# A four-layer decoder trunk on one core: residual stream moved by blocks, value projections made wide, and the steps of the layer joins handed out anew

## The chip, the cores and the metric

The kernel runs on one core of a Trainium2 chip. Its engines work side by side and meet through semaphores: TensorE (PE in the profile, its weight loads PEld), VectorE (DVE), ScalarE (ACT), GpSimd (POOL), and SyncE (SP), which issues most of the DMAs. The metric is device microseconds of one execution. Before the change three runs took 2686.42, 2691.14 and 2692.78 us; the median is 2691.14.

## What is computed

A sequence of 1024 positions, 1024 wide, goes through four layers. Each layer normalises, scales and shifts, runs one mixer, gates its output, and adds to the stream:

```
mod = (c @ ada_w[i] + ada_b[i])[:, None, :]
shift, scale, gate = jnp.split(mod, 3, axis=-1)
h = rmsnorm(x, norm_g[i]) * (1.0 + scale) + shift
y = hgrn2_mixer | swa_mixer | gdn_mixer      # i % 3, layers 0..3: hgrn2, swa, gdn, hgrn2
x = x + gate * y
```

Every mixer has one input projection, a branch output that is multiplied by a SiLU gate from the same projection, and one output projection. HGRN2 (layers 0 and 3) is a gated linear recurrence with 8 heads of 128, projections q, f, v, z of 1024 columns each. SWA (layer 1) is attention in a window of 128 with 16 query heads, 4 key heads and a sink for each head. GDN (layer 2) is a gated delta rule with a causal convolution of four taps on q, k and v and 16 value heads. All of it is float32, and a product of a projection is made of three matmuls on a high and a low part (`mm3`, L204 to L206: hi·hi, lo·hi, hi·lo).

## The kernel before, in words

Activations stand feature-major: a tile `x` holds one half of the sequence (512 positions) as eight blocks of 128 features by 512 positions. Nearly everything is done for half 0 and then for half 1 (`hf`). The normalised and modulated input is held as a pair `hhi`, `hlo`, again eight blocks a half. It comes from `norm_stats` (squares, a row sum on PE, an rsqrt on DVE, and `n_rb`, the factor spread over all partitions) and `norm_apply` (L504 to L506: for each of eight blocks one DVE product into `n_t`, one ACT add of the shift into `hhi`, one DVE step into `hlo`).

Weights come by SP in tiles `w_raw` of 256 KB with three buffers, which the streamed modulation weights `ada_w` share; ACT makes `w_hi` and DVE `w_lo`. `proj_fm` multiplies feature-major (result `proj_ps`, 24 matmuls of 512 columns for one half of 128 features). `proj_tm` multiplies position-major for the values (result `projt_ps`, matmuls of 256 columns, L204 to L206).

What sets the order is a scheduler. The program is written as generators, `weave` takes from several of them by the costs that they yield, some stretches have a raised priority (`early`, `high_priority`), and the scheduler then orders each engine's instructions, which the engine works off strictly in that order. While the mixer of head h runs (`mix`, `scan`, `inverse`: short dependent chains), the projections of the next head fill PE.

The stages touched by the change:

- **Prologue** (ends with the first `proj_ps` at 55 us): x is loaded and transposed on PE (`load_x`, L310), and the shift and scale of layer 0 are made from four 2 MB parts of `ada_w` by `ada_first`, all four parts on PE (`ada_row`, L400).
- **HGRN2 mix** (`mix`, L1030 to L1147): three levels of small matmuls (`lev_ps`, L1040, and L1087 for the last level), diagonal copies by POOL (L1081), the recurrence (`o_ps`, `s_ps`), then the head's output is transposed on PE by four matmuls (`ot_ps`, L1136), gated by `zs` on DVE (L1139), and stored to the scratch `od` by SP (L1141).
- **SWA mix**: the scores, softmax, transposes `pt_ps`, and pairs of `pv_ps` matmuls, one pair after each transpose (L1374).
- **GDN projections**: `conv` evicts a projection by an ACT copy (L644) and an ACT product (L648), three DVE taps (L650) and a tanh; `trans` transposes the result on PE at once.
- **Joins**: at the end of a layer `out_mm` and `rest` add into x (L1216, L534). After a half is added, its norm for the next layer is issued whole. Between layers a whole half of x goes to and from DRAM by SP in one DMA of 2 MB (`spill_x`, `fill_x`).

PSUM has eight banks; three of them (`proj` twice, `ta` once; two inside GDN) take projections in turn, `lev` has two, `tr`, `s` and `o` one each.

## Time and profile before

| what | value |
|---|---|
| median of three runs | 2691.14 us |
| the profiled execution, its own time | 2695.95 us |
| its span | 2694.2 us |
| instructions in the profile | 51458 |
| DMA traffic | 273.29 MB, mean 101 GB/s |

The prediction's sums are made against the profiled execution. In a row of the timeline the first number is the start in us from the span's start and the second the duration; matmuls are pipelined, so durations overlap, and what one costs in a stream is the distance between two starts. In a row of waits the numbers are total us, times, and the longest. In a row of stretches (`A:B`) come the length, then busy us of PE, PEld, DVE, ACT and POOL, the granted TensorE clock, the DMA share and GB/s. In a row of the groups by line come busy us and mean ns, then idle us before it and what ended that.

### The profile page before, as it was taken

How to read it: one execution, taken by the hardware profiler on the slowest of the kernel's cores; microseconds unless marked ns; L12 is line 12 of the kernel's file. 1: busy time of each engine (PE TensorE's matmuls, PEld its weight loads, DVE VectorE, ACT ScalarE, POOL GpSimd, SP SyncE). 2: the span in 40 equal slices, each digit the busy share in tenths (PEclk: the TensorE clock that was granted, in tenths of full speed). 3: DMA queues.
4: the chain of work that ended last, by engine and by line, in shares of the span. 5: the costliest groups of instructions: out<-in, count | busy, mean ns of one | idle time of the engine just before them, and what ended most of it. 6: DMA issues, size and time to landing. Idle time of an engine off the chain costs nothing.

```text
span 2694.2 us, 51458 instructions
## 1 busy us (share of the span) xinstructions
PE 2609.7 (97%) x18927; PEld 2102.4 (78%) x18927; DVE 2010.2 (75%) x5619; ACT 1272.9 (47%) x3268; POOL 136.7 (5%) x352
## 2 busy tenths in 40 slices
PE   8999999999999999999999999999999999999998
PEld 4878878778878777677877777777788878787877
DVE  6776766788687877777988888989876766656575
ACT  4333333444454655454556556666644433333342
POOL 0000100000000000001001101100000000000000
PEclk9999999999999999999999999999999999999999
DMA  6332222344223252333343333333584221111133
GB/s 241 92 93 84 68 79 72 110 137 157 59 87 103 75 158 91 114 98 84 102 115 99 96 105 100 94 97 82 179 254 132 71 60 37 56 51 43 49 118 115
DMA packets 361490, 273.29 MB, mean 101 GB/s; under 512 B 70499, under 2 KB 294166, under 8 KB 361238
## 3 DMA queue, kind: packets, MB, share of 16 engines
q1 hardware_dynamic: 360950, 268.96, 33.9%
q8 instruction: 149, 2.44, 0.4%
q14 instruction: 103, 0.84, 0.1%
q0 software_dynamic: 288, 1.05, 0.1%
HBM read 224.77 MB, written 45.15 MB: 100 GB/s over the span
## 4 chain that ended last, share of the span: by engine, by line
PE 71%; DVE 17%; DMA 5%; ACT 3%; issue 3%; SPq 1%; POOL 0%; DVEq 0%; ACTq 0%; POOLq 0%
PE proj_ps L206 10%; PE proj_ps L205 9%; PE proj_ps L204 9%; PE outp_ps L204 5%; PE outp_ps L205 5%; PE outp_ps L206 5%; DMA ada_w<-in_ada_w_dram 3%; PE projt_ps L204 3%; PE projt_ps L206 3%; PE projt_ps L205 3%; DVE w_lo L180 2%; DVE gd_tb L650 2%; PE pv_ps L1374 1%; DVE ada_acc L413 1%; PE w_ps L890 1%
## 5 line engine op out<-in xcount | busy, mean ns | idle before, releaser
L204 PE MATMUL proj_ps<-hhi,w_hi 128*128 128x512 f32 x1664 | 675.8, 406 | 6.1 <-ACT gd_tb L648 5.9
L206 PE MATMUL proj_ps<-hhi,w_lo 128*128 128x512 f32 x1664 | 679.9, 409 | 0.0
L205 PE MATMUL proj_ps<-hlo,w_hi 128*128 128x512 f32 x1664 | 671.2, 403 | 0.0
L204 PEld LDWEIGHTS proj_ps<-hhi,w_hi 128*128 128x128 f32 x1664 | 315.3, 190 | 59.4 <-ACT gd_tb L648 6.3
L205 PEld LDWEIGHTS proj_ps<-hlo,w_hi 128*128 128x128 f32 x1664 | 314.7, 189 | 59.0 <-issue 2.4
L206 PEld LDWEIGHTS proj_ps<-hhi,w_lo 128*128 128x128 f32 x1664 | 315.0, 189 | 56.1 <-issue 1.0
L179 ACT CAST w_hi<-w_raw 128x512 fp32r<-128x512 f32 x332 | 202.0, 611 | 303.3 <-PE proj_ps L205 188.1
L180 DVE TENSOR_TENSOR w_lo<-w_raw,w_hi 128x512 fp32r<-128x512 f32 x332 | 223.1, 674 | 155.2 <-ACT w_hi L179 129.1
L205 PE MATMUL projt_ps<-w_lo,hhi 128*128 128x256 f32 x896 | 258.7, 291 | 4.7 <-DVE w_lo L180 4.7
L204 PE MATMUL projt_ps<-w_hi,hhi 128*128 128x256 f32 x896 | 257.8, 290 | 0.6 <-ACT w_hi L179 0.6
L206 PE MATMUL projt_ps<-w_hi,hlo 128*128 128x256 f32 x896 | 256.8, 290 | 0.0
L204 PE MATMUL outp_ps<-o_hi,w_hi 128*128 128x512 f32 x576 | 229.2, 400 | 4.7 <-ACT o_hi L1200 3.4
L205 PE MATMUL outp_ps<-o_lo,w_hi 128*128 128x512 f32 x576 | 229.4, 399 | 0.0
L206 PE MATMUL outp_ps<-o_hi,w_lo 128*128 128x512 f32 x576 | 226.8, 396 | 0.7 <-DVE w_lo L183 0.7
L205 PEld LDWEIGHTS projt_ps<-w_lo,hhi 128*128 128x128 f32 x896 | 171.1, 192 | 8.1 <-DVE w_lo L180 6.0
L204 PEld LDWEIGHTS projt_ps<-w_hi,hhi 128*128 128x128 f32 x896 | 171.1, 192 | 3.7 <-ACT w_hi L179 1.0
L206 PEld LDWEIGHTS projt_ps<-w_hi,hlo 128*128 128x128 f32 x896 | 170.8, 192 | 2.4 <-issue 1.0
L650 DVE SCALAR_TENSOR_TENSOR gd_tb<-gd_xs,taps,gd_tb 128x512 f32<-128x512 f32 x192 | 145.2, 756 | 28.3 <-ACT gd_tb L648 19.7
L182 ACT ACTIVATE w_hi<-w_raw,par 128x512 fp32r<-128x512 f32 (+1 forms) x136 | 94.3, 698 | 137.0 <-PE outp_ps L205 89.2
L204 PEld LDWEIGHTS outp_ps<-o_hi,w_hi 128*128 128x128 f32 x576 | 108.8, 189 | 29.1 <-ACT o_hi L1200 4.9
L413 DVE SCALAR_TENSOR_TENSOR ada_acc<-ada_w,par,ada_acc 128x512 f32<-128x512 f32 x140 | 104.8, 749 | 33.4 <-DMA ada_w<-in_ada_w_dram 32.5
L206 PEld LDWEIGHTS outp_ps<-o_hi,w_lo 128*128 128x128 f32 x576 | 108.7, 189 | 23.5 <-DVE w_lo L183 1.3
(398 smaller groups left out, 4894.8 us busy)
## 6 DMA issues: line engine op xcount, KB each, us to landing
ada_w<-in_ada_w_dram SPq DMA_DIRECT2D x160, 256.0 KB, 2.8
w_raw<-in_hg_in_w_dram SPq DMA_DIRECT2D x136, 256.0 KB, 2.8
w_raw<-in_gd_in_w_dram SPq DMA_DIRECT2D x108, 256.0 KB, 3.0
o_in<-od SPq DMA_DIRECT2D x72, 256.0 KB, 3.2
w_raw<-in_gd_out_w_dram SPq DMA_DIRECT2D x64, 256.0 KB, 2.9
w_raw<-in_sw_in_w_dram SPq DMA_DIRECT2D x48, 256.0 KB, 2.9
w_raw<-in_hg_out_w_dram SPq DMA_DIRECT2D x40, 256.0 KB, 2.8
ada_w<-in_ada_w_dram SPq DMA_DIRECT2D x8, 1024.0 KB, 9.2
```

Of the source, the lines that this page charges most:

```text
L179: nc.scalar.copy(hi, raw)
L180: nc.vector.tensor_tensor(lo, raw, hi.bitcast(F32), ALU.subtract)
L182: nc.scalar.activation(hi, raw, AF.Copy, scale=scale)
L204: mm(out, a[0], b[0], start=start, stop=False)
L205: mm(out, a[0], b[1], start=False, stop=False)
L206: mm(out, a[1], b[0], start=False, stop=stop)
L413: self.nc.vector.scalar_tensor_tensor(acc, w, c, acc, ALU.mult, ALU.add)
L650: nc.vector.scalar_tensor_tensor(y, xs[:, j:j + HT], w(j), y, ALU.mult, ALU.add)
L890: nc.tensor.matmul(po[:, hd[a]], dd["u"][a, hf][:, cs], rhs, start=True, stop=True)
L1374: nc.tensor.matmul(po[a * 64:(a + 1) * 64], vg[:, n + 1 - nkb + b, :], p4[:, :, a, :], start=b == 0, stop=b == nkb - 1)
```

## The change

- **Values of HGRN2**: `proj_v` is made of two wide pieces of four heads each by `proj_wide` (matmuls of 512 columns, `projw_ps`) and no longer of four pieces by `proj_tm`. The values live in the two slots of x, which are free between the joins; head 7 has tiles of its own.
- **HGRN2 output**: for heads 0 to 6 the four PE transposes and the gating at once give way to a DVE product, a DVE transpose in squares of 32, four stores of 64 KB to a scratch `pd` that put the squares in place, and, in the next half's mix, a load from `pd`, a DVE product with `zs` and the store to `od` (`gate`).
- **HGRN2 last level**: L1087's twelve matmuls (widths 96, 64, 32) become sixteen (32, 64, 64, 32 on four column groups), issued together by `tied`; the diagonal copies move from POOL to ACT. Projections are spread one head to a mix, z of a head beside q and f of the next.
- **SWA**: both transposes come first, and the four `pv_ps` matmuls then run together. The k projection's two tile pairs share one rsqrt, and the order of the first projections changes.
- **GDN**: the transposes after a convolution wait for the middle of the next projection (`turns`); the gates z of units 1 and 2, half 0, are made at the layer's start, and the list `ZL` hands out the rest.
- **Norm**: `n_t` stands in PSUM (`lev`). The norm of half 1 at a join is no longer issued whole at the join but kept (`k.last`) and issued by the next layer: at its beginning in HGRN2 and SWA, and in GDN four blocks after each of the first two convolutions.
- **Stream by blocks**: each block of x is stored by POOL's queue as soon as it is added (`keep_x`), and loaded by SP in 256 KB blocks inside `out_mm` (`due`).
- **Prologue**: half 0 of x, the four `ada_w` parts and the first weights are requested in one order; parts 2 and 3 are multiplied on PE, parts 0 and 1 on DVE (`ada_first` with and without a bank); the norm of half 0 follows by halves of its blocks; the rotary tables move into layer 0's mix.

The difference, cut to its core:

```diff
     def norm_apply(self, i, hf, rb):
...
-            t = self.np.tile([P, HT], F32, name="n_t", tag="n_t", bufs=NB["n_t"])
+            t = self.psum("lev", "n_t", 2)
...
+            yield 1
...
     def conv(dd, hf, ps, ct, out):
...
-            nc.scalar.copy(xs[:, 3:], ps)
+            with self.tc.issue_after(self.hold.ins) if self.hold else nullcontext():
+                nc.scalar.copy(xs[:, 3:], ps)
...
+            self.piece = None
+            with self.tc.issue_after(last.ins):
+                drain(take(self.last, self.parts))
+            self.hold = self.piece
...
-        self.early(proj_kq(0, ds[0], ((0,),)), EV)
-        self.spill_x(1)
+        self.parts = 4
+        self.early(chain(proj_kq(0, ds[0], ((0,),)), proj_z(1, ds[1], (0,)), proj_z(2, ds[2], (0,))), EV)
+        drain(self.last)
...
+    def proj_wide(self, ws, evac, tts):
+        for tt in tts:
+            ps = self.proj_ps("projw_ps")
+            hf, ts = tt // 4, slice((tt % 4) * P, (tt % 4 + 1) * P)
+            for k in range(KT):
+                self.mm3(ps, (self.hhi[hf][:, k, ts], self.hlo[hf][:, k, ts]), ws[k], k == 0, k == KT - 1)
...
         def mix(h, d, halves=(0, 1)):
...
-                            nc.gpsimd.tensor_copy(at[gs, :, gs], A[gs].rearrange("p (c t) -> p c t", c=NC))
+                            nc.scalar.copy(at[gs, :, gs], A[gs].rearrange("p (c t) -> p c t", c=NC))
...
+                    if l == 3 and pend:
+                        gate()
...
                 if h < HA:
-                    nc.sync.dma_start(od[h * P:(h + 1) * P, hf * HT:(hf + 1) * HT], of)
+                    nc.vector.tensor_tensor(v4(on, "b c"), v4(po, "c b"), r[:, :, None, None].to_broadcast([P, NC, 4, 32]), ALU.mult)
+                    ob = tl("tmp")
+                    nc.vector.transpose(ob, on)
...
+                        nc.sync.dma_start(dst[a], ob[a * 32:(a + 1) * 32].rearrange("q (b t) -> q b t", b=4))
+                    pend.append((h, hf, d["zs", hf]))
...
+        def gate():
+            h, hf, z = pend.pop()
...
+            nc.sync.dma_start(t, self.pd[rows])
+            nc.vector.tensor_tensor(v4(z, "c b"), v4(t, "b c"), v4(z, "c b"), ALU.mult)
+            nc.sync.dma_start(od[rows], z)
...
     def out_mm(self, i, w_out, k0, nk, hf, scale=None, last=False):
...
+            if (hf, j) in self.due:
+                self.due.remove((hf, j))
+                self.nc.sync.dma_start(*self.block(hf, j))
...
+    def keep_x(self, hf, j):
+        if self.more:
+            x, d = self.block(hf, j)
+            self.nc.gpsimd.dma_start(d, x)
```

What the scheduler makes of it stands here at three places. The first is DVE at the join into GDN (layer 2), from the factor of half 1's norm (`n_sq`) on; `n_t` and `hlo` are norm blocks, `gd_tb<-gd_xs` the taps that belong to an eviction of a projection. Before, up to the first taps:

```order
L504 SCALAR_TENSOR_TENSOR n_t<-x_11280,gcol,n_rb 128x512 x2
L506 SCALAR_TENSOR_TENSOR hlo<-n_t,mod,hhi 128x512
L180 TENSOR_TENSOR w_lo<-w_raw,w_hi 128x512
L506 SCALAR_TENSOR_TENSOR hlo<-n_t,mod,hhi 128x512
L504 SCALAR_TENSOR_TENSOR n_t<-x_11280,gcol,n_rb 128x512 x2
L180 TENSOR_TENSOR w_lo<-w_raw,w_hi 128x512
L506 SCALAR_TENSOR_TENSOR hlo<-n_t,mod,hhi 128x512 x2
L504 SCALAR_TENSOR_TENSOR n_t<-x_11280,gcol,n_rb 128x512 x2
L180 TENSOR_TENSOR w_lo<-w_raw,w_hi 128x512
L506 SCALAR_TENSOR_TENSOR hlo<-n_t,mod,hhi 128x512 x2
L650 SCALAR_TENSOR_TENSOR gd_tb<-gd_xs,taps,gd_tb 128x512 x2
```

And with the change:

```order
L519 TENSOR_TENSOR n_sq<-ident,rs_y 128x512
L190 TENSOR_TENSOR w_lo<-w_raw,w_hi 128x512
L690 SCALAR_TENSOR_TENSOR gd_tb<-gd_xs,taps,gd_tb 128x512
L595 TENSOR_TENSOR gd_wab<-w_raw,gd_wab 128x8x32
L690 SCALAR_TENSOR_TENSOR gd_tb<-gd_xs,taps,gd_tb 128x512
L190 TENSOR_TENSOR w_lo<-w_raw,w_hi 128x512
L690 SCALAR_TENSOR_TENSOR gd_tb<-gd_xs,taps,gd_tb 128x512
L533 SCALAR_TENSOR_TENSOR n_t<-x_11000,gcol,n_rb 128x512 x2
L697 SCALAR_TENSOR_TENSOR gd_k<-gd_tb 128x512
L535 SCALAR_TENSOR_TENSOR hlo<-n_t,mod,hhi 128x512 x2
L533 SCALAR_TENSOR_TENSOR n_t<-x_11000,gcol,n_rb 128x512 x2
```

Sixteen norm steps stood ahead of the first taps; now the first taps stand ahead of them, and four blocks follow each of the first two convolutions.

The second place is PE in the prologue, between the first `ada_row` and the first wide value projection. Before:

```order
L400 MATMUL ada_row<-ada_w_362,par 1x512 x7
L400 MATMUL ada_row<-ada_w_383,par 1x512
L449 MATMUL ada_ps<-ones,ada_acc 128x1 x4
L400 MATMUL ada_row<-ada_w_383,par 1x512 x7
L310 MATMUL x_ps<-ident,x_in 128x128 x9
L449 MATMUL ada_ps<-ones,ada_acc 128x1 x4
L310 MATMUL x_ps<-ident,x_in 128x128 x23
L265 MATMUL taps_ps<-ident,taps_in 128x128
L204 MATMUL proj_ps<-hhi,w_hi 128x512
```

With the change, from the last matmuls of the first piece of q and f on:

```order
L218 MATMUL proj_ps<-hhi,w_hi 128x512
L219 MATMUL proj_ps<-hlo,w_hi 128x512
L220 MATMUL proj_ps<-hhi,w_lo 128x512
L428 MATMUL ada_row<-ada_w_182,par 1x512 x6
L480 MATMUL ada_ps<-ones,ada_acc 128x1 x4
L326 MATMUL x_ps<-ident,x_in 128x128 x8
L218 MATMUL projw_ps<-w_hi,hhi 128x512
L326 MATMUL x_ps<-ident,x_in 128x128 x4
```

The first 24 matmuls of the q and f projections now stand ahead of the second `ada_row` part and of the transposes of x's half 1, where all of these stood ahead of the first projection.

The third place is SP's queue in the first heads of layer 0, with the stores of a head's output, the loads of the streamed `ada_w`, and the weights. Before:

```order
L177 DMA w_raw<-in_hg_in_w_dram 128x4x128 x2
L427 DMA ada_w<-in_ada_w_dram 128x512 x3
L1141 DMA od_76<-hg_tmp 128x512
L427 DMA ada_w<-in_ada_w_dram 128x512 x2
L177 DMA w_raw<-in_hg_in_w_dram 128x4x128 x2
```

With the change:

```order
L1218 DMA pd<-hg_tmp 32x4x128 x4
L458 DMA ada_w<-in_ada_w_dram 128x512 x3
L1097 DMA hg_tmp<-pd 128x512
L458 DMA ada_w<-in_ada_w_dram 128x512
L187 DMA w_raw<-in_hg_in_w_dram 128x4x128 x2
L1099 DMA od_76<-hg_zs 128x512
```

One store has become four stores, a load that must follow them, and a store that follows a DVE product; weight loads stand behind them in the same queue.

More of the change, by code (lines that the diff above doesn't have):

```diff
@@ L100, in __init__ @@
         self.x = [None, None]
-        self.oo, self.pre = {}, {}
+        self.oo, self.pre, self.last, self.parts, self.due, self.more = {}, {}, iter(()), 0, set(), True
+        self.piece = self.hold = self.turn = self.step = None
     def hslot(self, name):
@@ new lines, in ada_load, with ada_first @@
+    def ada_load(self, i, part):
+        w = self.ins["ada_w"][i].rearrange("(k p) n -> p k n", p=P)
+        wk = self.hslot("ada_w0").bitcast(F32)
+        for g in range(2):
+            self.nc.sync.dma_start(wk[:, 4 * g:4 * g + 4, :], w[:, 4 * g:4 * g + 4, part * HT:(part + 1) * HT])
+        return wk
+    def ada_first(self, i, part, acc, wk, bank):
+        nc = self.nc
+        if bank:
+            pr = self.psum(*bank)
+            for k in range(KT):
+                nc.tensor.matmul(pr[0:1, :], self.cT[:, k:k + 1], wk[:, k, :], start=k == 0, stop=k == KT - 1)
+            acc = acc[0:1, :]
+            nc.scalar.copy(acc, pr[0:1, :])
+        else:
+            for k in range(KT):
+                self.ada_step(acc, wk[:, k, :], k)
+        yield
+        with self.tc.issue_after(self.step.ins) if self.step else nullcontext():
@@ L1028, in mix @@
             for hf in halves:
[L1029 removed]
+                q, f, kg, qf = (d[x, hf] for x in ("q", "f", "kg", "qf"))
+                v = value(h, hf)
                 k0 = d["k0", hf]
@@ L1150, in hgrn2 @@
         ds = [dict() for _ in range(H)]
+        drain(self.last)
         gv = proj_v(0)
-        self.early(chain(proj(0, ds[0], "qf", (0,)), take(gv, 8)))
+        if i == 0:
+            for g, at, n, ew in ((proj(0, ds[0], "qf", (0,)), self.start[0], 80, EW), (take(gv, 16), self.start[1], 0, 50)):
+                self.early(g, eo=self.tc.cur_priority - at + n, ew=ew)
+            rst = ExitStack()
+            rp = rst.enter_context(self.tc.tile_pool(name="rope", bufs=1, reuse_waits="tile"))
+            side = chain(take(side, 18), self.rope_tables(rp), side)
+        else:
+            self.early(chain(proj(0, ds[0], "qf", (0,)), take(gv, 16)))
+        if i == 0:
+            self.spill_x(1)
         drain(chain(gv, proj(0, ds[0], "qf", (1,))))
```

388 lines of the change are left out of this document (219 added, 169 removed).

## The prediction

> **What bounds the kernel now.** I read first the page's busy times and chain, then the stretches, then the waits of PE, and last the rows at the places that the change touches.
>
> ```profile
> PE 2609.7 (97%) x18927; PEld 2102.4 (78%) x18927; DVE 2010.2 (75%) x5619; ACT 1272.9 (47%) x3268; POOL 136.7 (5%) x352
> ...
> PE 71%; DVE 17%; DMA 5%; ACT 3%; issue 3%; SPq 1%; POOL 0%; DVEq 0%; ACTq 0%; POOLq 0%
> ```
>
> PE is busy in 2609.7 of 2694.2 us. All its idle time is 84.5 us, so no mending of waits alone can bring more than that, and a larger gain must come out of PE's own work. In the stretches the columns are the length, then busy us of PE, PEld, DVE, ACT, POOL, the granted clock, the DMA share and GB/s:
>
> ```profile
> 0.00:55.10 55.10, 45.84 (x166) 18.89 (x166) 29.93 (x108) 23.24 (x41) 3.91 (x43) 0.97 0.80 285
> ...
> 1131.00:1137.40 6.40, 0.54 (x3) 0.12 (x2) 6.40 (x11) 4.58 (x8) 0.67 (x2) 0.77 0.34 87
> 1137.40:1150.00 12.60, 12.50 (x48) 8.28 (x48) 6.77 (x10) 5.23 (x19) 2.25 (x10) 0.84 0.25 63
> 1200.00:1900.00 700.00, 685.84 (x4766) 549.94 (x4765) 607.62 (x1738) 422.60 (x1331) 59.05 (x147) 0.99 0.37 98
> 2130.00:2580.00 450.00, 445.46 (x4241) 372.47 (x4241) 286.95 (x968) 163.71 (x389) 29.10 (x64) 1.00 0.16 48
> 35.00:40.00 5.00, 5.00 (x13) 1.02 (x14) 4.54 (x8) 2.71 (x4) 0.00 (x0) 1.00 1.05 389
> ```
>
> In layer 3 (2130 to 2580) PE is idle in 4.5 of 450 us while DVE has 163 us free and ACT 286: what leaves PE there leaves the time. In GDN (1200 to 1900) DVE is at 87%, so work moved to DVE is no longer free. The prologue is another regime: DMA at 389 GB/s and PE busy at once. The longest wait of a projection is at a join, 1131 to 1137:
>
> ```profile
> PE proj_ps L204 <- ACT gd_tb L648: 5.9, 1, 5.9
> PE ot_ps L1136 <- DVE hg_tmp L1132: 5.6, 11, 1.3
> PE projt_ps L205 <- DVE w_lo L180: 4.7, 5, 1.4
> ...
> PE vtr_ps L658 <- DVE gd_tb L652: 1.4, 4, 0.7
> PE qtr_ps L658 <- DVE gd_q L652: 1.3, 4, 0.4
> ...
> PE ktr_ps L658 <- DVE gd_k L652: 1.3, 2, 1.0
> ```
>
> **The change part by part.** *Prologue.* The chain of waits up to the first projection (start, length):
>
> ```profile
> 6.00 8.36 DMA ada_w<-in_ada_w_dram
> 14.41 3.11 PE ada_row L400 x4
> ...
> 27.17 6.96 PE ada_row L400 x16
> ...
> 55.21 0.40 PE proj_ps L204
> ```
>
> PE multiplies four parts of `ada_w`, 6.96 us for 16 passes or 0.435 each, and the first projection starts at 55.2. With the change 32 of these passes leave PE (13.9 us), and 16 DVE steps take their place, where DVE has 25.2 us free in these 55. The first projection no longer waits for all four parts: x's half 0 (2 MB), two parts (4 MB) and the first weights (1 MB) come first, 7 MB. At 0.389 MB per us that is 18 us after 6.0, and with the norm of four blocks behind them (four DVE products and four `hlo` steps of 0.75 us, 6 us) the first projection starts at about 30. It then starves: the other parts and the norm's second half come by 45 to 49, and the 24 matmuls of a piece last 5.5 us. I take 16 us as gain: the 13.9 us of PE work and a little of the idle 9.3 in this stretch. The low end is 6 (the DMAs for 8 MB of `ada_w`, 2 MB of x and the weights stay, about 30 us at that rate, and the pieces wait for them), the high end 24 (55 less 30).
>
> *Wide values.* 1536 matmuls of 256 columns become 768 of 512. The first and last rows of two unbroken streams, of nine narrow and fifteen wide ones:
>
> ```profile
> 71.00 0.28 PE L204 MATMUL projt_ps<-w_hi,hhi 128*128 128x256 f32 x1
> ...
> 71.96 0.28 PE L205 MATMUL projt_ps<-w_lo,hhi 128*128 128x256 f32 x1
> ...
> 2211.06 0.39 PE L205 MATMUL proj_ps<-hlo,w_hi 128*128 128x512 f32 x1
> ...
> 2214.24 0.39 PE L204 MATMUL proj_ps<-hhi,w_hi 128*128 128x512 f32 x1
> ```
>
> Eight pitches in 0.96 us are 0.120 each, fourteen in 3.18 are 0.227. Two narrow ones thus take 0.240 and one wide one 0.227, and 768 × 0.013 = 10 us, between 8 and 12 by the rounding of the rows. The Trainium skill ("TensorE: Matmul & The Clock Gate", section "Back-to-back issue gap") gives the time of a matmul as its columns over 2.4 GHz and a gap of 2.5 ns, which by an estimate would save 2.5 ns a pair or 2 us in all. The rows above show more than the page for both widths, 0.120 and 0.227, so the row decides, and the sum goes by 10.
>
> *Transposes of HGRN2's output.* 28 of 32 groups of four leave PE. In layer 3:
>
> ```profile
> 2208.79 0.39 PE L205 MATMUL proj_ps<-hlo,w_hi 128*128 128x512 f32 x1
> 2209.43 0.63 PE L1136 MATMUL ot_ps<-ident,hg_tmp 128*128 128x128 f32 x4 [0.26 <-DVE hg_tmp L1132]
> 2209.82 0.48 PE L206 MATMUL proj_ps<-hhi,w_lo 128*128 128x512 f32 x1
> ...
> 2219.97 0.39 PE L205 MATMUL proj_ps<-hlo,w_hi 128*128 128x512 f32 x1
> 2220.29 0.85 PE L1087 MATMUL lev_ps<-hg_X,hg_kg 128*32 128x96 f32 x24
> 2221.07 0.50 PE L206 MATMUL proj_ps<-hhi,w_lo 128*128 128x512 f32 x1
> ```
>
> From one projection matmul to the next are 1.03 us, less the usual 0.23 makes 0.80, of which 0.26 is a wait: 0.54 without it, × 28 = 15. The waits bring 5.6 × 28/32 = 4.9 more, if no other takes their place. I take 18, low 9.8 (the group's 0.63 less the 0.28 that one matmul lasts, 0.35 × 28), high 20.
>
> *Last level.* A group interrupts the stream for 1.10 − 0.23 = 0.87 us (2219.97 to 2221.07). The widest column group of 32 falls from 96 to 64 columns while the others run beside it. A third of the 0.78 us from 2220.29 to 2221.07 is 0.26, × 32 groups = 8.3. There are 128 more matmuls to issue, so I take 6, low 0, high 9.
>
> *SWA's values.* In layer 1:
>
> ```profile
> 786.30 0.28 PE L205 MATMUL projt_ps<-w_lo,hhi 128*128 128x256 f32 x1
> 786.60 0.65 PE L1374 MATMUL pv_ps<-sw_pth,v 128*64 128x256 f32 x4
> 787.18 0.66 PE L1368 MATMUL pt_ps<-ident,sw_sm 128*128 128x128 f32 x4
> ```
>
> Four `pv_ps` start 0.30 after a projection matmul instead of 0.12, so a switch costs 0.18, and the four hold PE 0.58. Two of them together save one or two switches, about 0.3 us, in 28 blocks that have two keys' blocks: 8, I take 6, low 0, high 9.
>
> *Joins.* At 1131.06 the last free bank is full, and the eviction by ACT stands behind the sixteen DVE and eight ACT steps of half 1's norm: PE loses 5.9 us, and the clock of 0.84 in the next 12.6 us costs 12.6 × (1 − 0.84/0.98) = 1.8. The wait for `w_lo`, 4.7 in five times, is made mostly at the join into SWA (waits of PE from 600 to 720):
>
> ```profile
> PE projt_ps L205 <- DVE w_lo L180: 4.2, 4, 1.4
> ```
>
> There too it stands behind such steps. Together 5.9 + 1.8 + 4.2 = 11.9, of which I take 12. The order on DVE shows the first taps ahead of the norm's blocks now, but four blocks follow at one stroke behind each of two convolutions. If each stroke (4 × 2 × 0.75 = 6 us of DVE) stalls a projection fully, the 12 come back: low 0. High 16, with the shorter waits at the other joins.
>
> *Turns.* Transposes in the middle of the next projection end the waits of `ktr_ps`, `qtr_ps` and `vtr_ps`, 4.0 us: 3, between 4 gained and 3 lost (a switch in the middle of a projection where before one stood at its end).
>
> *What is added.*
>
> ```profile
> L859 DVE STREAM_TRANSPOSE gd_of<-gd_of 128x512 f32<-128x512 f32 x32 | 22.5, 704 | 0.1
> L1139 DVE TENSOR_TENSOR hg_tmp<-ot_ps,hg_zs 128x512 f32<-128x512 f32 x32 | 21.9, 685 | 1.7 <-PE ot_ps L1136 1.7
> L1090 ACT COPY hg_at<-lev_ps 32x256 f32<-32x256 f32 x32 | 11.6, 364 | 0.4
> od<-gd_of SPq DMA_DIRECT2D x128, 64.0 KB, 1.8
> o_in<-od SPq DMA_DIRECT2D x72, 256.0 KB, 3.2
> ```
>
> DVE gets 28 squares' transposes of 0.70 and 28 products of 0.69, 39 us over two layers, against 163 free in one of them. ACT gets 128 diagonal copies from POOL, at most 0.36 each, 47 us, against 286. PE's work hides both; without that cover they cost 86 us. SP gets 112 stores and 28 loads for `pd` and the blocks of x. Work beside PE still delays some short chain, so I take 5 us lost, 0 to 15 (a third of a microsecond in each of 28 heads and halves makes 9).
>
> The sum: 16 + 10 + 18 + 6 + 6 + 12 + 3 − 5 = 66. The profiled execution took 2695.95, so 2630; it stands 4.8 above the median of 2691.14, and so I predict **2625 us**. All low ends together (24 gained, 18 given back) would give 2685 beside the median, all high ends (94) 2597.
>
> **The rivals.** *The gaps grow back.* In a layer where PE is at 99%, the short chains may set the pace: when the transposes go, the mix waits for `hg_tmp` (5.6 us in 11 waits now) at another place. Then only bare work leaves: 13.9 of `ada_row`, 10 of the values, 9.8 of transposes, and of the rest 5: 39, time 2652. For it speak 85 us of idle time that are spread thin; against it, that DVE and ACT have more than a third free in HGRN2. Chance 0.18.
>
> *A larger gain:* the high ends of prologue, transposes and joins (24 + 20 + 16 in place of 46) and 11 of the small ones' 14: about 2600. For it speaks that each of these places waits now; against it, that eight terms would have to fall on one side. Chance 0.12.
>
> *The queue of SP (slower).* Each of 28 loads from `pd` must follow its stores (1.8 us to land) and then takes 3.2, in the same queue as the weight tiles. It decides once the wait is longer than what `w_raw`'s three buffers cover. Half a projection of 24 matmuls (5.5 us) uses two tiles. If each round trip of 1.8 + 3.2 is exposed, 28 × 5.0 = 140 are lost, if only the load, 28 × 3.2 = 90: then 2625 + 90 = 2715, slower. Against it speaks the row on which the cover rests, that weights are cast early and ACT waits for PE to release them:
>
> ```profile
> ACT w_hi L179 <- PE proj_ps L205: 188.1, 133, 4.6
> ```
>
> 133 waits of 1.4 us mean in which the next weight had already landed. Chance 0.06.
>
> *The queue of POOL.* Blocks of x are stored by POOL's queue, and its transfers took longer than SP's:
>
> ```profile
> rope_sw_qnorm<-cg_sw_qnorm POOLq DMA_DIRECT2D x1, 512.0 KB, 7.1
> ...
> rq<-rope_sw_qnorm SPq DMA_DIRECT2D x1, 512.0 KB, 3.8
> ```
>
> If the slot of x is held until a store has landed 7 us late, at three joins 3 × 7.5 = 23 are lost: 2648. The Trainium skill ("SBUF — State Buffer", section "SBUF: two separate sides") says that descriptors of a DMA issued from GpSimd are written by GpSimd's own cores, which are locked out while DVE runs a two-port operation; it would lengthen these stores, and no row here shows such a case. Chance 0.05.
>
> *It doesn't do what it says:* the new waits eat all that leaves PE, time within 8 us of 2691. Chance 0.04, as PE loses 784 matmuls on balance (1536, 112 and 32 gone, 768 and 128 added), whatever else comes.
>
> **How the numbers follow.** The forecast has 0.55. Faster: 0.55 + 0.18 + 0.12 + 0.05 = **0.90**; within 0.3% (8 us, about what a measurement of this kernel can tell) **0.04**; slower **0.06**. The half widths of the terms, added as squares (9, 2, 5, 5, 5, 8, 4, 8), make 17, so the forecast alone goes from 2608 to 2642. The range of **2590 to 2665** holds it, the first rival and that of POOL's queue with 13 us to spare, and the larger gain, with 7 us below all high ends for edits that no term prices (the k projections' shared rsqrt, and GDN's gates made ahead); it leaves out the queue of SP, no change, and what lies beyond the low ends of several terms at once.
>
> **What would show it.** In the profile after: the first projection at about 30 and the first wide value matmul about 16 us sooner than the first `projt_ps` now; 28 fewer groups `ot_ps`, and layer 3 with PE idle still under 2%; `projw_ps` at a pitch of 0.227; no single wait of 5.9 at GDN's start. I am wrong if PE's idle time grows past 100 us: in HGRN2 with `w_raw` or `pd` as the releaser (SP), at the joins with x (POOL), or at GDN's start with the convolution's evictions behind the blocks of the norm, each stall there followed by a clock under 0.9.

## The result, and the profile after

The changed kernel takes 2665.53 us (median of four runs, 2664.74 to 2670.69) against 2690.11 beside it: a ratio of 0.991, 95% interval 0.9898 to 0.9922. It is faster, by 24.6 us where 66 were forecast, and lies half a microsecond outside the range. Timed again on another chip it took 2662.28 (ratio 0.9896, 0.9879 to 0.9912); the mean of the two ratios, 0.9903, is the base below, and 0.001 of ratio is 2.7 us.

The page of the changed kernel, its engines and its chain:

```profile
PE 2568.7 (96%) x18271; PEld 2046.2 (77%) x18271; DVE 2021.6 (76%) x5655; ACT 1323.5 (50%) x3467; POOL 105.7 (4%) x278
...
PE 72%; DVE 14%; DMA 6%; ACT 5%; issue 2%; SPq 1%; DVEq 0%; ACTq 0%
```

PE's busy time fell by 41.0 us (2609.7 to 2568.7), but its idle time grew from 84.5 to 95.4 (2664.1 less 2568.7). The waits of PE, those that answer to the rows before:

```profile
PE z_ps L883 <- DVE gd_uq L878: 7.4, 7, 1.7
PE outp_ps L218 <- ACT o_hi L1314: 7.0, 3, 3.4
PE ada_row L428 <- DMA ada_w<-in_ada_w_dram: 5.3, 2, 5.0
...
PE proj_ps L218 <- ACT gd_tb L688: 3.3, 4, 1.6
...
PE s_ps L1473 <- DVE hlo L535: 2.6, 1, 2.6
```

The single wait of 5.9 us for `gd_tb` is gone. New are 5.3 us for `ada_w` in the prologue, and 2.6 us in which SWA's scores (`s_ps`) wait for a step of a norm, which they had never met before.

Where the time went by layers shows in the last matmul of each layer's output projection (first number of a row: its start). First the kernel before, from a second profile taken of it later, whose execution lies near its median; then the changed one:

```profile
629.96 0.40 PE L206 MATMUL out_ps<-hg_f,w_lo 128*128 128x512 f32 x1
...
1108.71 0.39 PE L206 MATMUL out_ps<-sw_of,w_lo 128*128 128x512 f32 x1
...
2114.67 0.39 PE L206 MATMUL outp_ps<-o_hi,w_lo 128*128 128x512 f32 x1
...
2678.18 0.40 PE L206 MATMUL out_ps<-hg_f,w_lo 128*128 128x512 f32 x1
```

```profile
615.32 0.40 PE L220 MATMUL out_ps<-hg_f,w_lo 128*128 128x512 f32 x1
...
1104.55 0.40 PE L220 MATMUL out_ps<-sw_of,w_lo 128*128 128x512 f32 x1
...
2101.32 0.39 PE L220 MATMUL outp_ps<-o_hi,w_lo 128*128 128x512 f32 x1
...
2653.28 0.40 PE L220 MATMUL out_ps<-hg_f,w_lo 128*128 128x512 f32 x1
```

The differences of neighbours are the layers' lengths:

| stage | before, us | changed, us | difference | forecast |
|---|---|---|---|---|
| prologue and layer 0 (HGRN2) | 630.0 | 615.3 | −14.6 | about −30 |
| layer 1 (SWA) | 478.8 | 489.2 | +10.5 | about −10 |
| layer 2 (GDN) | 1006.0 | 996.8 | −9.2 | about −11 |
| layer 3 (HGRN2) | 563.5 | 552.0 | −11.5 | about −15 |

The last column spreads the terms of the sum over the layers in which they lie (wide values, transposes, the last level and the added work by halves over layers 0 and 3, the join of 11.9 as 7.7 in GDN and 4.2 in SWA). Two stages failed: the first one by 15 us, and SWA, which became slower. How much slower varies: in the profiles below in which nothing of SWA or of the norms is edited, layer 1 lasts between 482.9 and 490.1, so 4 to 11 more than the 478.8 before.

### The profile page after: what moved, and what is told of

It reads as the page before. It is cut to its first block, busy times and chain, and to the rows that moved or that the text cites. A ratio compares the mean times of both kernels' runs of the same rounds, so it can differ in the third digit from the quotient of the medians.

```text
span 2664.1 us, 50723 instructions
## 1 busy us (share of the span) xinstructions
PE 2568.7 (96%) x18271; PEld 2046.2 (77%) x18271; DVE 2021.6 (76%) x5655; ACT 1323.5 (50%) x3467; POOL 105.7 (4%) x278
## 4 chain that ended last, share of the span: by engine, by line
PE 72%; DVE 14%; DMA 6%; ACT 5%; issue 2%; SPq 1%; DVEq 0%; ACTq 0%
PE proj_ps L218 10%; PE proj_ps L220 10%; PE proj_ps L219 10%; PE outp_ps L218 4%; PE outp_ps L219 4%; PE outp_ps L220 4%; PE projw_ps L219 2%; PE projw_ps L218 2%; PE projw_ps L220 2%; DVE gd_tb L690 1%; DVE w_lo L190 1%; PE projt_ps L219 1%; PE projt_ps L220 1%; PE pv_ps L1502 1%; PE projt_ps L218 1%
## 5 line engine op out<-in xcount | busy, mean ns | idle before, releaser
L220 PE MATMUL proj_ps<-hhi,w_lo 128*128 128x512 f32 x1664 | 671.1, 403 | 0.0
L189 ACT CAST w_hi<-w_raw 128x512 fp32r<-128x512 f32 x352 | 214.5, 612 | 270.5 <-PE proj_ps L219 150.8
L190 DVE TENSOR_TENSOR w_lo<-w_raw,w_hi 128x512 fp32r<-128x512 f32 x352 | 236.5, 676 | 138.2 <-ACT w_hi L189 135.2
L193 DVE SCALAR_TENSOR_TENSOR w_lo<-w_raw,par,w_hi 128x512 fp32r<-128x512 f32 (+1 forms) x136 | 96.9, 715 | 45.2 <-ACT w_hi L192 43.9
L444 DVE SCALAR_TENSOR_TENSOR ada_acc<-ada_w,par,ada_acc 128x512 f32<-128x512 f32 x154 | 114.9, 746 | 19.8 <-DMA ada_w<-in_ada_w_dram 18.8
L219 PEld LDWEIGHTS outp_ps<-o_lo,w_hi 128*128 128x128 f32 x576 | 109.4, 190 | 24.9 <-DVE o_lo L1315 3.0
L219 PE MATMUL projt_ps<-w_lo,hhi 128*128 128x256 f32 x384 | 111.6, 292 | 2.2 <-DVE w_lo L190 2.2
L218 PE MATMUL projt_ps<-w_hi,hhi 128*128 128x256 f32 x384 | 111.0, 292 | 2.7 <-ACT w_hi L189 2.7
L220 PE MATMUL projt_ps<-w_hi,hlo 128*128 128x256 f32 x384 | 111.4, 292 | 0.0
L218 PE MATMUL projw_ps<-w_hi,hhi 128*128 128x512 f32 x256 | 102.8, 407 | 2.3 <-DVE hg_q L1032 2.3
```

Of the source, the lines that this page charges most:

```text
L189: nc.scalar.copy(hi, raw)
L190: nc.vector.tensor_tensor(lo, raw, hi.bitcast(F32), ALU.subtract)
L193: nc.vector.scalar_tensor_tensor(lo, raw, scale, hi.bitcast(F32), ALU.mult, ALU.subtract)
L218: mm(out, a[0], b[0], start=start, stop=False)
L219: mm(out, a[0], b[1], start=False, stop=False)
L220: mm(out, a[1], b[0], start=False, stop=stop)
```

## The experiments

All but the last are edits of the changed kernel, timed beside the kernel before. What counts is the distance of a ratio from the base of 0.9903. Intervals reach 0.0009 to 0.0017 to either side, 2 to 5 us, and the base has one of its own, so effects under 4 us are told as none that could be measured.

### The prologue

Undone first was the work that left PE: all four parts of the modulation weights on TensorE again.

```diff
-(0, None, D), (3, ("s", "ada_row", 1), None), (1, None, None)
+(0, ("lev", "ada_row", 2), D), (3, ("s", "ada_row", 1), None), (1, ("s", "ada_row", 1), None)
```

> The changed kernel, but with the two parts of the modulation weights that DVE took over (0 and 1) multiplied by TensorE again: 32 ada_row passes back on PE (13.9 us at 0.435), 16 DVE steps gone; everything else of the prologue stays. Theory A (the forecast's term: what leaves PE in the prologue leaves the time): about 14 us slower than the changed kernel's 2665.5, so 2679. Theory B (PE stands idle for about 19 us of the first 75 and waits there for transfers and DVE, so the passes cost nothing where they lie): 2664 to 2668, and PE's busy time between 0 and 75 us grows by the passes.

Measured 2663.11, ratio 0.9899 (0.9884 to 0.9913): no slower. The stretches of 25 us from 25 on, of the changed kernel and then of this one (columns as before: PE, PEld, DVE, ACT and POOL busy, the granted clock, DMA share, GB/s):

```profile
25.00:50.00 25.00, 19.34 (x65) 9.76 (x65) 13.26 (x23) 10.03 (x17) 0.00 (x0) 0.79 0.94 356
50.00:75.00 25.00, 20.14 (x79) 14.91 (x79) 19.93 (x46) 14.08 (x24) 0.98 (x2) 0.80 0.40 133
```

```profile
25.00:50.00 25.00, 23.99 (x74) 8.91 (x73) 7.61 (x15) 9.80 (x17) 0.00 (x0) 0.93 0.94 358
50.00:75.00 25.00, 21.66 (x99) 14.73 (x98) 17.42 (x41) 15.13 (x27) 0.98 (x2) 0.94 0.36 126
```

With 32 more passes PE is busy for 6.2 us more in the same 50 us, at a clock of 0.93 and 0.94 instead of 0.79 and 0.80. PE had been idle there, and what work it had ran slower. The passes had cost nothing that the end of the prologue would notice, and taking them away gained nothing.

Next, 2 MB fewer to load: the last part (number 1) is computed from a tile that is there already, which leaves one load out. By its code this is the tile of part 0 (`ada[1]`), the second one requested, and not the third's as the expectation says; the bytes that are saved are the same.

```diff
-k.ada_load(layers[0], part), bank
+k.ada_load(layers[0], part) if part != 1 else ada[1][3], bank
```

> The changed kernel without the load of the fourth part of the first modulation weights (2 MB fewer; that part is computed from the third part's tile, so the output is wrong). At 0.389 MB/us these are 5.2 us of transfers. Theory B1 (the prologue ends when the transfers do): 4 to 6 us faster than 2665.5, about 2660, and the second half of the first q and f pieces starts at about 52 instead of 57.7. Theory B2 (the chain of x's transposes, ACT's evictions and DVE's steps behind the transfers sets the end): within 1.5 us of 2665.5.

Measured 2662.59, ratio 0.9905 (0.9888 to 0.9921): no effect. In its trace the second half of the first pieces starts at 56.99, in the changed kernel at 57.72, so the bytes don't set it either. The chain of waits of the changed kernel shows what does:

```profile
48.05 0.60 PE x_ps L326 x4
48.68 0.59 ACT x L329
49.32 0.77 PE x_ps L326 x4
50.11 0.58 ACT x L329
...
54.30 1.07 PE ada_ps L480 x8
55.61 0.67 PE x_ps L326 x4
56.31 0.59 ACT x L329
56.95 1.12 PE x_ps L326 x4
```

In PE's order the transposes of x's half 1 stand ahead of the last `ada_ps` and of the second half of the first pieces, and they are paced by evictions that only ACT makes now. Each link is short, and all stand in one row.

Last, the order of before in the changed kernel (the requests of x and the place of the rotary tables stay as changed; the line that puts all four parts on PE is not shown): four parts on PE ahead of the norm, the norm whole, x's half 1 through the projections' banks with evictions by ACT and DVE in turn, the first projections without their own place.

```diff
-        a = k.norm_apply(layers[0], 0, rb)
-        for n in range(2):
-            gs = [k.ada_first(*x) for x in ada[2 * n:2 * n + 2]]
...
+        for x in ada:
+            drain(k.ada_first(*x))
+        drain(k.norm_apply(layers[0], 0, rb))
...
-                pt = self.psum(("tr", "s")[g], "x_ps", 1) if hf else self.proj_ps("x_ps")
+                pt = self.proj_ps("x_ps")
...
-                (nc.scalar.copy if hf or n % 2 else nc.vector.tensor_copy)(dst, src)
+                (nc.scalar.copy if n % 2 else nc.vector.tensor_copy)(dst, src)
```

> The changed kernel with the prologue's order of the kernel before: all four parts on TensorE ahead of the norm, the norm of half 0 whole, x's half 1 transposed through the projections' banks and evicted by ACT and DVE in turn, the first projections without their own place in the order. Forecast's term: 16 us more than the changed kernel. Theory B (what sets the start is the chain behind the weights' parts, which reaches the second half of the first pieces at 57 us in every form so far): within 4 us of the changed kernel, faster or slower.

Measured 2661.30, ratio 0.9886 (0.9871 to 0.9901), beside 0.9896 for the changed kernel on the same chip. Its stretch, and its first projection:

```profile
50.00:75.00 25.00, 25.00 (x110) 19.66 (x111) 23.33 (x48) 17.26 (x30) 0.00 (x0) 1.00 0.50 170
...
50.47 0.50 PE L218 MATMUL proj_ps<-hhi,w_hi 128*128 128x512 f32 x1
```

The first projection comes 15.7 us later than in the changed kernel (50.47 against 34.75), and nothing is lost: from 50 to 75 us PE is busy without a gap at a granted clock of 1.00, and layer 0 ends at 610.1 instead of 615.3. The early start bought 24 matmuls (5.5 us) and gaps behind them.

The base was timed again with these:

> The changed kernel unchanged, timed beside the next three on one chip, as the base of their comparisons: 2665.5, between 2660 and 2670 on every theory.

2662.28, as told above.

### HGRN2: transposes, values, last level

```diff
                 if h < HA:
...
+                    pt = self.psum("tr", "ot_ps", 1)
+                    for c in range(NC):
...
+                        nc.tensor.transpose(pt[:, cs], on[:, cs], self.ident)
...
+                    nc.vector.tensor_tensor(of, pt, d["zs", hf], ALU.mult)
+                    nc.sync.dma_start(od[h * P:(h + 1) * P, hf * HT:(hf + 1) * HT], of)
+                elif h < 0:
                     nc.vector.tensor_tensor(v4(on, "b c"), v4(po, "c b"), ...)
```

> The changed kernel with the four TensorE transposes and the gating at once for all heads of HGRN2 again (no squares, no scratch pd); everything else stays. Bare work: 112 transposes at 0.109 us are 12.2 us more, 2665.5 + 12 = 2677. The forecast's term (with what a group interrupts and with its waits): 18 us more, 2683. Rival (the stores, the load and the later gate cost elsewhere what the transposes saved): within 4 us of 2665.5, or faster.

Measured 2684.53, ratio 0.9984 (0.9974 to 0.9994): 0.0081 above the base, 22 us. Beside the bare 12 stand the wait for `hg_tmp`, which the forecast had counted, and a longer wait for `hg_X` (3.5 us in the changed kernel), which it had not:

```profile
PE lev_ps L1116 <- DVE hg_X L1139: 7.6, 16, 1.4
PE ot_ps L1215 <- DVE hg_tmp L1211: 6.9, 16, 1.2
```

This one edit is worth nearly all that the whole change gained.

```diff
-            for k in range(KT):
-                self.mm3(ps, ..., ws[k], k == 0, k == KT - 1)
+            for n in (slice(0, 256), slice(256, HT)):
+                for k in range(KT):
+                    self.mm3(ps[:, n], ..., [w[:, n] for w in ws[k]], k == 0, k == KT - 1)
```

> The changed kernel with every wide matmul of HGRN2's values cut in two of 256 columns (1536 for 768; weights, order and eviction as in the change). Forecast's term: 768 x 0.013 = 10 us more, 2675. Rival (in the mix's gaps the narrow ones lose nothing): within 4 us of 2665.5.

Measured 2674.32, ratio 0.9946 (0.993 to 0.9962): 0.0043, 11.6 us, where 10 were forecast. In the traces layer 3 is 4.3 us longer with the narrow ones (556.3 against 552.0), half of it.

The old last level (three column groups, three evictions), and the diagonal copies on POOL again:

```diff
-                        self.tied([lambda c=c, m=m: mm(c, *m) for c in range(NC) for m in (...)])
+                          for c in range(NC):
+                            for g in range(3):
+                                nc.tensor.matmul(pl[gs, c, g + 1:, :], kg[...], xv[...], start=True, stop=True)
```

> The changed kernel with the last level's matmuls (96, 64 and 32 columns, three column groups) and their three evictions as before; the diagonal copies stay on ACT. Forecast's term: 6 us slower than the changed kernel (pooled ratio 0.990), so a ratio of about 0.9925. By the accounting of pitch (2 us in each of the two layers): 4 us slower. Rival (sixteen matmuls and a fourth ACT copy cost what the width saves): within 2 us, ratio 0.989 to 0.991.

Measured 2664.36, ratio 0.9905 (0.9892 to 0.9919): no effect that could be told; the interval leaves out the 6 us and ends at the 4. Yet the saving is there in PE's stream. A group of the last level between two projection matmuls in layer 3, first with the old matmuls, then in the changed kernel:

```profile
2129.08 0.39 PE L219 MATMUL projw_ps<-w_lo,hhi 128*128 128x512 f32 x1
2129.40 0.85 PE L1164 MATMUL lev_ps<-hg_X,hg_kg 128*32 128x96 f32 x24
2130.18 0.50 PE L220 MATMUL projw_ps<-w_hi,hlo 128*128 128x512 f32 x1
```

```profile
2185.69 0.40 PE L218 MATMUL proj_ps<-hhi,w_hi 128*128 128x512 f32 x1
2186.01 0.65 PE L1161 MATMUL lev_ps<-hg_X,hg_kg 128*32 128x32 f32 x32
2186.59 0.50 PE L219 MATMUL proj_ps<-hlo,w_hi 128*128 128x512 f32 x1
```

The interruption is 0.90 us long instead of 1.10. Over 32 groups that is 6.4 us, the forecast's 6; layer 3 is 2.0 us longer with the old matmuls (554.0 against 552.0), layer 0 by 0.4, and the total shows none of it. Where the rest goes stays open.

```diff
-                            nc.scalar.copy(at[gs, :, gs], A[gs].rearrange(...))
+                            nc.gpsimd.tensor_copy(at[gs, :, gs], A[gs].rearrange(...))
```

> The changed kernel with the 128 diagonal copies of the last level on POOL again (0.47 us each there, 0.29 on ACT). Forecast (the copies on ACT are hidden): within 2 us of the changed kernel. Rival (ACT's 38 us more lie in the short chains of the mix): 4 to 8 us faster, ratio 0.987 to 0.9885.

Measured 2672.28, ratio 0.9938 (0.9926 to 0.9951): 9 us slower. That contradicts both: the copies on ACT are not merely hidden, in the changed mix they are needed. The group of the copies, and what waits for them, in that kernel:

```profile
L1157 POOL COPY hg_at<-hg_A 32x128 f32<-32x128 f32 x128 | 71.7, 560 | 826.0 <-DVE hg_A L1152 553.4 <-DVE hg_F L1172 165.3 <-DVE rs_t L172 33.1
...
PE o_ps L1194 <- POOL hg_at L1157: 9.1, 5, 2.0
...
L1157 POOL COPY hg_at<-hg_A x64: 284/455/3259, 2130.4 to 2559.1; 32x128 f32<-32x128 f32 x64
```

Before the change no such wait stands among PE's, with the same copies on POOL at 0.47 us each. In this kernel half of them take under 0.46 too, but six groups of four take 4.5 to 5.3 us, and the last row, of layer 3 alone, gives the shortest, the median and the longest copy: 284, 455 and 3259 ns; in all six DVE works without a gap meanwhile. That DVE holds POOL up is a guess from this coincidence. Layer 3 is 564.3 us long here, 12.3 more than in the changed kernel and as long as before the change (563.5). So the move keeps a new wait from coming; whether it would gain anything in the kernel before was not run.

### SWA's matmuls together, GDN's transposes, the stores of x

```diff
-                self.tied([lambda b=b, a=a: nc.tensor.matmul(po[a * 64:(a + 1) * 64], ..., start=b == nkb - 1, stop=b == 0) ...])
+                    for a in range(2):
+                        nc.tensor.matmul(po[a * 64:(a + 1) * 64], ..., start=b == 0, stop=b == nkb - 1)
```

> The changed kernel with SWA's pv_ps matmuls in pairs after each transpose again. Forecast's term: 6 us more, 2671. Rival (TensorE's stream of projections fills both forms alike, and the accounting of pitch showed no gain): within 3 us of 2665.5.

Measured 2667.10, ratio 0.9916 (0.9903 to 0.9929): 0.0013 or 3.5 us, with an interval from nothing to 7 us, not told from none; layer 1 is 490.0 us long, in the changed kernel 489.2 and 486.2 in its two profiles.

```diff
                 self.turn = evac(hf, ps)
+                self.turns()
```

> The changed kernel with GDN's transposes at once after each convolution. Forecast's term: 3 us slower. If these transposes are what removed the stall at GDN's start: 8 to 11 us slower, with a wait on the eviction at 1110 to 1140. Rival: within 2 us, no such wait.

Measured 2665.93, ratio 0.9911 (0.9897 to 0.9926): 2 us, not told from none; no wait on the eviction at GDN's start.

```diff
-            self.nc.gpsimd.dma_start(d, x)
+            self.nc.sync.dma_start(d, x)
```

> The changed kernel with the stores of x's blocks issued in SP's queue instead of POOL's. Rival of the forecast (POOL's queue holds the slots of x): up to 23 us faster at the three joins. Theory (nothing waits for these stores, SP's weight loads are delayed a little instead): within 4 us of the changed kernel.

Measured 2661.14, ratio 0.9889 (0.9874 to 0.9904): not to be told from none. In the changed kernel the blocks' stores land in 2.9 us on POOL's queue (2.1 on SP's in this run), and not in the 7 that the rival had feared:

```profile
xd<-x POOLq DMA_DIRECT2D x48, 256.0 KB, 2.9
```

### The joins

First the norm of half 1 whole at each join, then also the gates z no longer ahead:

```diff
-                if hf == 0:
-                    drain(a)
-                else:
-                    k.last = a
+                drain(a)
+                if hf == 1:
+                    k.last = iter(())
                     k.nst.close()
```

> The changed kernel with the norm of half 1 issued whole at each join, as in the kernel before; the stream by blocks and the gates z made ahead stay. Forecast's term: the stall at GDN's start (5.9 us and the slow clock behind it) and the waits at SWA's start come back, 2665.5 + 12 = 2677. Rival (the eviction that stalled is reached in time because the gates made ahead and the blocks moved the work, or the stall only moves to another place): within 3 us of 2665.5.

Measured 2661.76, ratio 0.9903 (0.9889 to 0.9918): no effect, and no wait on the eviction at GDN's start. The norm's pieces, which the forecast had made the reason for 12 us, are worth nothing in this kernel. Whether they would have ended the stall with `n_t` still in SBUF, where it stood before, no run shows.

```diff
-        self.early(chain(proj_kq(0, ds[0], ((0,),)), proj_z(1, ds[1], (0,)), proj_z(2, ds[2], (0,))), EV)
+        self.early(proj_kq(0, ds[0], ((0,),)), EV)
...
+ZL = ((2, 0, 1),), ((3, 0, 1),), ((4, 0, 1),), ((5, 0, 1),), ((6, 0),), ((6, 1),), ((7, 0, 1),), ()
```

> The changed kernel with the norm of half 1 whole at the joins and GDN's gates z of units 1 and 2 no longer made ahead (the old list). The norm whole alone gave no stall at GDN's start. Theory Z (the gates made ahead took the stall away, the norm's pieces had no part): the stall of about 6 us on the eviction and the slow clock behind it come back at 1110 to 1140 us, 8 to 12 us more, about 2674. Rival (something else of the change, such as transposes that wait for the middle of the next projection, took it away): no wait over 2 us there, within 4 us of 2665.5.

Measured 2665.00, ratio 0.9909 (0.9896 to 0.9922), with no wait over 2 us there: the theory of the gates falls too. Yet the stall of 5.9 us is gone in every one of these kernels.

The other end of the same join, where SWA's last half still runs beside the norm of half 0, gave the lead. In the changed kernel the norm's `n_t` stands in the two PSUM banks `lev`, in which SWA's scores stand as well. DVE in the changed kernel around the wait of 2.6 us, and the stretch in which SWA's last blocks run after the output projection that covered them is used up:

```profile
1047.79 1.40 DVE L533 SCALAR_TENSOR_TENSOR n_t<-x,gcol,n_rb 128x512 f32<-128x512 f32 x2
1049.77 1.40 DVE L535 SCALAR_TENSOR_TENSOR hlo<-n_t,mod,hhi 128x512 fp32r<-128x512 f32 x2
...
1075.00:1092.00 17.00, 11.13 (x49) 6.72 (x48) 7.07 (x22) 6.80 (x16) 0.00 (x0) 0.76 0.12 32
```

PE is idle for 5.9 of these 17 us, and its clock falls to 0.76. With `n_t` of half 0 in SBUF at this join:

```diff
-            t = self.psum("lev", "n_t", 2)
+            t = self.psum("lev", "n_t", 2) if hf or i != 2 else self.np.tile([P, HT], F32, name="n_t", tag="n_t", bufs=NB["n_t"])
...
+NB = {"n_acc": 1, "n_sq": 2, "n_t": 1}
```

> The changed kernel with n_t of half 0 at the join into GDN in SBUF (one buffer) instead of the two PSUM banks that SWA's scores use. In the profile of the changed kernel the scores of SWA's last half wait 2.6 us for the norm's hlo at 1047 us, and the tail of SWA's mix stands uncovered from 1077 to 1092 (8.6 us of stalls). Theory: the banks shared with n_t delay the mix, 3 to 8 us faster, 2658 to 2662. Rival (the tail is uncovered for another reason, the wait costs nothing): within 1.5 us of 2665.5.

Measured 2656.74, ratio 0.9874 (0.986 to 0.9889): 8 us faster than the base. Layer 1 is 475.7 us long instead of 489.2 and 486.2, and in the three other runs below with this edit 474.0 to 479.2, so this gain is no accident of one profile. The stretch that answers to the one above:

```profile
1066.00:1084.00 18.00, 15.92 (x79) 10.75 (x78) 9.46 (x19) 8.30 (x19) 0.54 (x1) 0.91 0.28 78
```

And what had taken GDN's stall away was the same edit at half 1. Among ACT's instructions the first eviction of GDN (`gd_xs`) stands behind all steps `hhi` of half 1's norm where `n_t` is in SBUF, and among them where it is in PSUM. The end of the eight steps with `n_t` in SBUF for both halves (norm whole; the run is told below):

```profile
1118.22 0.72 ACT L534 ACTIVATE hhi<-n_t,mod 128x512 fp32r<-128x512 f32 x1 [1.60 <-DVE n_t L533]
1120.54 0.72 ACT L534 ACTIVATE hhi<-n_t,mod 128x512 fp32r<-128x512 f32 x1 [1.60 <-DVE n_t L533]
1121.17 0.57 ACT L684 COPY gd_xs<-proj_ps 128x512 f32<-128x512 f32 x1
```

With `n_t` in PSUM (norm whole as well), the first two steps stand between two evictions:

```profile
1110.41 0.58 ACT L684 COPY gd_xs<-proj_ps 128x512 f32<-128x512 f32 x1
...
1112.50 1.35 ACT L534 ACTIVATE hhi<-n_t,mod 128x512 fp32r<-128x512 f32 x2 [0.92 <-DVE n_t L533]
1114.33 0.58 ACT L684 COPY gd_xs<-proj_ps 128x512 f32<-128x512 f32 x1
```

The run with both halves in SBUF also has the norm whole, as in the first run of this section:

```diff
-            t = self.psum("lev", "n_t", 2)
+            t = self.psum("lev", "n_t", 2) if i != 2 else self.np.tile([P, HT], F32, name="n_t", tag="n_t", bufs=NB["n_t"])
...
+NB = {"n_acc": 1, "n_sq": 2, "n_t": 1}
```

> The changed kernel with n_t of both halves in SBUF (one buffer) at the join into GDN, and the norm of half 1 whole. Theory (GDN's tiles take over the SBUF that the norm's pool held, so the first eviction must wait for the last norm step; n_t in PSUM took the stall away and put another on the scores): the scores' wait at 1047 us is gone as in the run with half 0 alone, and a wait of about 6 us on the eviction at GDN's start is back with a slow clock behind it; against that run (ratio 0.9874) 8 to 11 us slower, 0.9905 to 0.9915. Rival: no wait over 2 us at GDN's start, ratio 0.987 to 0.988.

Measured 2668.54, ratio 0.9918 (0.9905 to 0.9932), 0.0044 or 12 us slower than with half 0 alone. Its waits from 1010 to 1165:

```profile
PE proj_ps L218 <- ACT gd_tb L688: 11.5, 1, 11.5
...
PE s_ps L1473 <- ACT sw_sm L1485: 1.3, 1, 1.3
```

The wait at GDN's start is back (11.5 us with one buffer, where the kernel before had two and waited 5.9), and layer 2 is 1011.9 us long against 993.4 with half 0 alone, and against 996.2 with the norm whole and `n_t` in PSUM. That the place of `n_t` decides is thus shown. Why is not: the theory's reason, that GDN's tiles take over the norm's memory, was not measured apart, and one row of this run speaks against it for the tile of the first eviction. POOL writes the first columns of `gd_xs` at 1093.8, 9 us before the norm's first step at 1103.2:

```profile
L678 POOL MEMSET gd_xs<- x2: 108/109/110, 1093.8 to 1093.8; 128x3 f32 x2
```

### Together

> The changed kernel with the two edits together that went the right way: n_t of half 0 at the join into GDN in SBUF, and all four parts of the first modulation weights on TensorE. If their gains are separate (9 and 2 to 3 us): 11 to 12 us faster than the changed kernel, about 2654. If the second was chance: 9 us faster, 2657.

Measured 2654.92, ratio 0.9866 (0.9852 to 0.9881), 7.4 us faster than the changed kernel on the same chip: the gain of `n_t` alone. This is the fastest median of all, 35 us below the kernel before.

> n_t of half 0 at the join into GDN in SBUF, the four parts on TensorE, and the diagonal copies on POOL. If the copies on ACT cost nothing: as the first two edits alone, ratio 0.9866. If they cost 4 to 8 us: ratio 0.984 to 0.985.

Measured 2667.47, ratio 0.992 (0.9908 to 0.9933): 0.0054 or 14.5 us above the two edits alone. The copies on POOL cost here too, and take the gain away again.

> The kernel before, unchanged: a ratio of 1 with its interval. If its first profile was of a slow execution, the lengths of its four layers differ from the first ones (631, 481, 1008 and 564 us) by some 4 to 8 us in all, and show in which stages.

2689.91, ratio 0.9995 (0.9986 to 1.0004). Its second profile spans 2688.1 us, 6.1 less than the first; the layers differ by 1.2, 1.8, 2.3 and 0.8 us, so no single place was slow. A sum against one profiled execution carries such a difference.

## Why the prediction was wrong

It named the bound, the sign and the largest term rightly, and was wrong in the size by a factor of 2.7.

- **Transposes of HGRN2's output:** forecast 18, undone 22. The row of interruptions was the right price: beside the matmuls, the switches and the waits of the stream. The wait for `hg_X`, which the sum left out, makes 4 more.
- **Wide values:** forecast 10, undone 11.6. The distance of starts in the trace held.
- **Prologue, the step that failed first:** "I take 16 us as gain: the 13.9 us of PE work and a little of the idle 9.3". The rows were read rightly and the conclusion was wrong. Before the change the passes stood in the chain of waits; once they were gone, the chain went over weight loads, DVE and ACT, and PE stood idle: in the first 75 us for 19.2 us, where it had been 9.3. The forecast itself had noted that the pieces starve until 45 to 49, and priced the passes all the same. Undone, the passes cost nothing, and neither does the old order; with it layer 0 ends 5.2 us sooner in the trace. The first projection came at 34.75 (forecast about 30), and PE lost what it gained in gaps and in the slow clock behind them. Not even the low end of 6 was low enough.
- **Joins, the second step that failed:** "Together 5.9 + 1.8 + 4.2 = 11.9, of which I take 12", by the norm's pieces. The 5.9 did go, but in this kernel through `n_t`'s place in PSUM, an edit the sum doesn't name at all; the same edit made SWA's scores and the norm of half 0 share two banks, which cost 8 us at the other end of the same join. The waits for `w_lo` at SWA's start did not go: 1.9 us for it and 2.7 for `w_hi` from 560 to 720 in the changed kernel. The 7.7 that were expected in GDN, less SWA's 8, leave nothing of the 12.
- **Last level and SWA's values:** forecast 6 each, measured none for the first and 3.5 for the second, with an interval that holds none. The price of the last level was right in PE's stream (0.20 us a group), and still the time did not follow; the step from the stream to the time failed there.
- **Turns:** forecast 3, measured 2 with an interval that holds both.
- **Added work:** 5 lost was an estimate that no run measures as a whole. Its part of the diagonal copies, priced as ACT work that PE hides, has the other sign in the changed kernel: on POOL again they cost 9 us.
- **The rivals:** the time fell nearest to "the gaps grow back" (2652, 0.18), and PE's idle time did grow; but the gaps are not spread over HGRN2's chains, they stand in the prologue and at SWA's end. The queue of SP (slower, 2715) did not show: no wait for `pd` or `w_raw` of the changed kernel is among PE's longer ones. The queue of POOL did not show either.

The terms that showed when they were undone (22, 11.6, 9, 3.5 and 2) add up to 48, where the change gained 26 at the base. In layer 3 alone the transposes, the values and the copies make 9.7, 4.3 and 12.3 us by their own runs, and the layer became 11.5 shorter. So the terms don't add up: each was undone in a kernel that holds all others, where one undone edit opens waits for another (the copies on POOL show it). Which of them overlap stays open.

## What to carry to other kernels

Before pricing work that leaves the busiest engine, look what that very stretch waits for once the work is gone: where loads or short chains come next, the work may have cost nothing. When a buffer moves to another memory, list who else uses the new place at that time, and read the order on the engines again; here this one line, `n_t`, was worth more in each direction than the reordering around it. An early start of a stage is worth only what can be done before the next thing it waits for.

## What was not expected of the hardware

A gap costs more than itself. After the 5.0 us in which PE waited for `ada_w`, the passes ran at half speed for about 7 us (a row of the timeline, then stretches, of the changed kernel):

```profile
28.97 1.86 PE L428 MATMUL ada_row<-ada_w,par 128*1 128x512 f32 x2 [5.00 <-DMA ada_w<-in_ada_w_dram]
...
30.00:35.00 5.00, 4.65 (x12) 2.12 (x12) 2.19 (x5) 1.26 (x2) 0.00 (x0) 0.50 1.06 389
35.00:40.00 5.00, 5.00 (x20) 4.10 (x21) 4.83 (x8) 2.80 (x5) 0.00 (x0) 0.89 1.03 408
50.00:55.00 5.00, 4.05 (x19) 2.76 (x18) 4.44 (x12) 2.28 (x4) 0.00 (x0) 0.68 0.38 118
55.00:60.00 5.00, 4.07 (x18) 3.24 (x18) 4.36 (x10) 2.72 (x5) 0.98 (x2) 0.66 0.00 0
```

Two passes took 1.86 us, where two of sixteen took 0.87 before. The Trainium skill ("TensorE: Matmul & The Clock Gate", section "What's actually happening") tells of a clock that falls to one half after an idle window of about 3.4 us and rises after as much of sustained work; the granted clock of 0.50 agrees. A slow clock also went with shorter gaps that came one after another: from 50 to 60 us no gap in PE's rows is over 1 us, and the mean clock was 0.66 to 0.68.
